# A hybrid decoder trunk: SBUF buffers shared out anew, S5 products on another engine, one weight sum formed later

## The chip, the core and the metric

The kernel runs on one core of a Trainium2 chip. The metric is the device time of one execution in microseconds; three runs were taken. TensorE (PE) does the matmuls, VectorE (DVE) and ScalarE (ACT) the element-wise work, GpSimd (POOL) some more of it, and SyncE (SP) issues most of the DMAs, in one queue and in program order.

## The reference, cut to what matters

One layer: one projection of x, (1024, 2048), to all branches, three mixers, and one projection back, with a residual and LayerNorm.

```python
h = jnp.einsum('bld,dn->bln', x, w_in[l])
(s5_u, s5_z, ml_qk, ml_v, ml_i, ml_f, ml_o, ml_z, ssd_xbc, ssd_dt, ssd_z) = split_in(h)
y_s5 = s5_mixer(s5_u, ...) * jax.nn.silu(s5_z.astype(f32))
qk = jax.nn.silu(causal_dwconv(ml_qk, ml_conv_w[l], ml_conv_b[l]))
y_ml = mlstm_mixer(q, k, ml_v, ...) * jax.nn.silu(ml_z.astype(f32))
xbc = jax.nn.silu(causal_dwconv(ssd_xbc, ssd_conv_w[l], ssd_conv_b[l]))
y_ssd = rms_norm(ssd_mixer(xs, bs, cs, ...) * jax.nn.silu(ssd_z.astype(f32)), ssd_norm_g[l])
mixed = jnp.concatenate([y_s5, y_ml, y_ssd], axis=-1)
x = layer_norm(DEEPNORM_ALPHA * x + jnp.einsum('bln,nd->bld', mixed, w_out[l]), ln_g[l], ln_b[l])
```

The S5 mixer is a complex diagonal recurrence over time, s(t) = lam_bar * s(t-1) + B u(t), computed here in batches of states with complex numbers as pairs of real rows.

## The kernel before, in words

**Products.** Every fp32 operand of a projection is split in two fp32r parts: `split` (L178 to L180) casts it on ScalarE (names ending in h) and subtracts on VectorE (names ending in l). A product takes three matmuls: h by h, h by l, l by h. A weight tile is `w<n>`, numbered in the order of use: raw `w<n>r`, parts `w<n>h` and `w<n>l`.

**The block** (`block`, about 0 to 720 us) does a part of the input projection by a scheme of block products over the two halves of rows and of contraction, of Strassen's kind: seven products instead of eight, on sums of blocks. First come the token-major weights, in five stages, (1), (2), (5, 6), (3, 7) and (4), for three groups of columns of which the first and third are `w_gt`. A stage's piece is `unit` (L1371): one weight tile of 256 rows, two steps k of 128 rows, four tiles of tokens, 24 matmuls of 128x512. After it come the channel-major weights `w_c` (the columns, about 480 to 720 us), in the order `CSEQ`. Weights w24 to w31 are the first group's of stage (5, 6), w72 to w75 the same group's in stage (4). Operand sums of x (`xc`, `xd`, `xe`, parts `p..`) are formed beside them, and `tick` puts other work between units: the S5 mixer's constants and then its eight batches `s5m0` to `s5m7` (`s5_batch`, L1040), one step of a generator at a time.

**Weight sums.** A sum is a `Chain`: `raw` loads the first block (`w24r`), `mix` (L231) loads another (`w24q`) and adds or subtracts it on VectorE in place. `right` (L1169) says which blocks each product needs. With `early` true, product 6's chain subtracts a further block after its split and stores the result in DRAM (`tg`), from where product 4 takes it ready; with `early` false the store comes before, and product 4 loads tg and the further block and subtracts there. Before, `early` is true for the first of the three groups (`g == 0`).

**Buffers.** All raw loads, weights, sums and operands alike, take turns in `NR` = 5 buffers ("wr", 4 KB per partition), which a load may enter once the buffer's last reader is done. Tiles made by `gt` take turns in `NG` = 24 buffers of 2 KB ("g"). Both pools last for the whole kernel. The block's accumulators lie in `zp`, 23 buffers of 2 KB, and the 24th takes one of "g" (L1294).

**Order.** Each engine takes its instructions in the order in which the program's builder put them, and the builder places them by when it thinks buffers and data come free: the counts of buffers shift the order on every queue, SP's above all.

**After the block** come two halves of the tokens (`half`: conv, mLSTM, SSD), and an output projection after each, whose second operand is loaded as `y0r` and `y1r` through the same raw buffers, one per weight tile at first. x's second half is loaded as `x1r`.

Of the kernel before, what the change touches and what calls it, by code (L numbers as in the profile page):

```python
# [17 lines left out]
P = 128  # L18
# [6 lines left out]
QSC = 96.0 ** -0.5  # L25
NEG = -1.0e30
NWARM = 8
NG = 24
NR = 5


_W = dict(ssd_conv_w=56, ssd_conv_b=14, ml_conv_w=24, ml_conv_b=6, ssd_d=6, ssd_norm_g=6, ml_norm_g=6, s5_b_glu=4, s5_lre=32, s5_lim=32, s5_lst=32)
# [7 lines left out]
def hybrid_trunk(ctx: ExitStack, tc: tile.TileContext, a: dict, out: bass.AP, dbg=None):  # L40
# [3 lines left out]
    cp = ctx.enter_context(tc.tile_pool(name="cp", bufs=1))  # L44
    xp = ctx.enter_context(tc.tile_pool(name="xp", bufs=8))
    wp = ctx.enter_context(tc.tile_pool(name="wp", bufs=3))
    gp = ctx.enter_context(tc.tile_pool(name="gp", bufs=NG))
    pj = ctx.enter_context(tc.tile_pool(name="pj", bufs=4, space=PSUM))
    mx = ctx.enter_context(tc.tile_pool(name="mx", bufs=4, space=PSUM))
    dr = ctx.enter_context(tc.tile_pool(name="dr", bufs=1, space=DRAM))  # L50
# [6 lines left out]
    def gt(name, shape=(P, HT), dtype=F32):  # L57
        return gp.tile(list(shape), dtype, name=name, tag="g")
# [109 lines left out]
    bg = Background()  # L168


    warm = gt("warm", dtype=BF16)
    dve.memset(warm, 0.0)
    wps = mx.tile([P, HT], F32, name="warmp", tag="mx")
    for _ in range(NWARM):
        pe.matmul(wps, lhsT=warm[:, 0:P], rhs=warm, start=True, stop=True)
# [6 lines left out]
    class Tokens:  # L182
# [5 lines left out]
        def load(self, kk):  # L188
            assert kk == len(self.h)
            if self.early:  # L190
                self.load_early(kk)
                return
            r = wp.tile([P, 2, HT], F32, name=f"{self.nm}r{kk}", tag="wr", bufs=NR)
            sync.dma_start(out=r, in_=self.src(kk))
            th = xp.tile([P, 2, HT], F32R, name=f"{self.nm}h{kk}", tag="xh")
            tl = xp.tile([P, 2, HT], F32R, name=f"{self.nm}l{kk}", tag="xl")
            split(r, th, tl)
            self.h.append(th)
            self.l.append(tl)
# [13 lines left out]
            self.l.append(tl)  # L213

    def raw(src, shape, n):
        r = wp.tile(list(shape), F32, name=n, tag="wr", bufs=NR)
        sync.dma_start(out=r, in_=src)
        return r

# [15 lines left out]
    class Weights:  # L235
# [34 lines left out]

        def begin(self):
            src, shape = self.plan[self.at]
            r = wp.tile(list(shape), F32, name=f"w{self.at}r", tag="wr", bufs=NR)
            self.first = src, (r, *self.parts())
            self.ready.append(self.first[1][1:])

# [762 lines left out]
    def s5_batch(sb, gT, ctx_):  # L1039
        n = f"s5m{sb}"  # L1040
        bt, hf = sb // 2, sb % 2

        def ld(nm):
            t_ = gt(n + nm)
            sync.dma_start(out=t_, in_=s5d[nm][sb])
            return t_

        def ld_half(nm, r0):

            t_ = gt(n + nm)  # L1050
# [24 lines left out]
        for g in range(4):
            pe.matmul(A[:, g * P:(g + 1) * P], lhsT=R[:, g * P:(g + 1) * P], rhs=U[:, g * P:(g + 1) * P], start=True, stop=True)
        As = gt(n + "As")
        act.mul(As[0:64], A[64:128], -1.0)
        act.copy(out=As[64:128], in_=A[0:64])
        v, v2 = gt(n + "v"), gt(n + "v2")  # L1080
        dve.tensor_mul(out=v, in0=A, in1=T0)
        pool.tensor_mul(out=v2, in0=As, in1=T1)
        dve.tensor_add(out=v, in0=v, in1=v2)
        w = gt(n + "w")
        dve.tensor_tensor_scan(out=w, data0=rt.rearrange("p q j -> p (q j)"), data1=v, initial=0.0, op0=ALU.mult, op1=ALU.add)
        yield
        ws = gt(n + "ws")
        act.mul(ws[0:64], w[64:128], -1.0)
        act.copy(out=ws[64:128], in_=w[0:64])
        x1, x2, X = gt(n + "x1"), gt(n + "x2"), gt(n + "X", (P, 4, P))  # L1090
        v3 = lambda t_: t_.rearrange("p (q j) -> p q j", q=4)[:, :, 0:P - 1]
        dve.tensor_mul(out=x1, in0=w, in1=T0)
        pool.tensor_mul(out=x2, in0=ws, in1=T1)
        pool.memset(X[:, :, 0:1], 0.0)
        dve.tensor_sub(out=X[:, :, 1:P], in0=v3(x1), in1=v3(x2))
        O = ld("O")
        M = gt(n + "M", (P, 8, 64))
        K = s5d["K"]
        for t in range(8):
            sync.dma_start(out=M[:, t, :], in_=K[16 * t:16 * t + P, 64 * sb:64 * sb + 64])  # L1100
        yield
        yield
        ps = pm(n + "y")
        for g in range(4):
            sl = slice(g * P, (g + 1) * P)
            pe.matmul(ps[:, sl], lhsT=X[:, g, :], rhs=O[:, sl], start=True, stop=False, skip_group_check=True)
            pe.matmul(ps[:, sl], lhsT=U[:, sl], rhs=M[:, :, 16 * g:16 * g + 16], start=False, stop=True, skip_group_check=True)
        if hf == 0:
            ctx_["Y"] = [gt(n + f"Y{i}", (P, 4, P)) for i in range(2)]
        Y = ctx_["Y"]  # L1110
        for i in range(2):
            act.copy(out=Y[i][:, :, 64 * hf:64 * hf + 64].rearrange("p t (g c) -> p g t c", g=4),
                     in_=ps.rearrange("p (g t c) -> p g t c", g=4, t=8)[:, :, 4 * i:4 * i + 4, :])
        yield
        if hf == 1:

            for i in range(2):
                ps = pm(n + f"g{i}")
                for x in range(4):
                    pe.transpose(ps[:, (3 - x) * P:(4 - x) * P], Y[i][:, x, :], ident)  # L1120
                lo = 4 - 4 * i
                for h in range(2):
                    act.activation(out=gT[bt][h].rearrange("p (j t) -> p t j", t=8)[:, lo:lo + 4, :],
                                   in_=ps.rearrange("p (t j) -> p t j", t=4)[:, :, 64 * h:64 * h + 64], func=AF.Gelu_apprx_tanh)
            yield
# [65 lines left out]

    w_t = [lambda c, u, g=g: a["w_gt"][g, c, u] for g in range(2)]
    w_t.insert(1, lambda c, u: a["w_gv"][c, u])
    wt = [[right(lambda k, c, g=g, u=u: w_t[g](c, 4 * k + u), (P, 2, GN[g]), f"tg{g}{u}", g == 0) for u in range(4)] for g in range(3)]
    wc = [right(lambda k, c, p=p: a["w_c"][p[c], k], (P, 8, P), f"cg{p[0]}", j > 2) for j, p in enumerate(GC)]
    STAGES = ((1,), (2,), (5, 6), (3, 7), (4,))

# [94 lines left out]
    def block():  # L1292
# [6 lines left out]

        def new(n):  # L1300
            count.append(n)
            return gt(n) if len(count) == 24 else zp.tile([P, HT], F32, name=n, tag="state")

        def plus(o, x, y, op=add):
            dve.tensor_tensor(out=o, in0=x, in1=y, op=op)  # L1305
# [65 lines left out]
        def unit(i, X, g, u, ps, w):  # L1371
            wh, wl = w
            N = GN[g]
            order = [(t, k) for t in range(4) for k in range(2)] if u in (0, 3) else [(t, k) for k in range(2) for t in range(4)]
            for t, k in order:
                K = 2 * u + k
                s_h, s_l = X.h[u][:, k, t * P:(t + 1) * P], X.l[u][:, k, t * P:(t + 1) * P]
                pe.matmul(ps[t][:, 0:N], lhsT=s_h, rhs=wh[:, k, :], start=(K == 0), stop=False)
                pe.matmul(ps[t][:, 0:N], lhsT=s_h, rhs=wl[:, k, :], start=False, stop=False)
                pe.matmul(ps[t][:, 0:N], lhsT=s_l, rhs=wh[:, k, :], start=False, stop=(K == 7))  # L1380
                if K == 7:
                    evac_t(i, g, t, ps[t])
            tick()
# [231 lines left out]

    mixsrc = lambda h: lambda kk: mixT[kk * 256:(kk + 1) * 256, h * HT:(h + 1) * HT].rearrange("(two p) n -> p two n", p=P)
    X = [Tokens(lambda kk, h=h: a["xT"][h, kk], f"x{h}") for h in range(2)] + [Tokens(mixsrc(h), f"y{h}") for h in range(2)]
    with tc.tile_pool(name="zp", bufs=23) as zp:
        X[0] = block()
    sp = ctx.enter_context(tc.tile_pool(name="sp", bufs=2))  # L1620
    hp = ctx.enter_context(tc.tile_pool(name="hp", bufs=1))
    st_s = hp.tile([P, 768], F32, name="st_s")
# [96 lines left out]
```

## Time and profile before

| | |
|---|---|
| median of three runs | 1634.3 us (1633.9 to 1637.83) |
| the profiled execution | 1636.77 us, span 1634.8 us |
| mean granted clock of TensorE | 0.988 |
| busy: PE, DVE, ACT, POOL | 97%, 68%, 40%, 6% of the span |
| DMA | 333.56 MB, mean 204 GB/s |

The page's busy shares say which engine fills the span. The windows say, by stretch, how long each engine was busy and which clock TensorE was granted. The list of waits names the instruction for which an engine stood, and what it stood for. The timeline gives single instructions in order, with the idle time before each in brackets.

### The profile page before, as it was taken

Reading aid. Unit: us, or ns where it says so; the run is one execution under the profiler, and the core shown is the slowest. Engines: PE = TensorE matmul, PEld = TensorE weight load, DVE = VectorE, ACT = ScalarE, POOL = GpSimd, SP = SyncE. Lnnn points to the kernel's source line nnn. Section 1 sums busy time; section 2 is a strip of 40 time slices with the busy share of each in tenths; the row PEclk is TensorE's granted clock in tenths of the full one; section 3 lists DMA queues with packets and bytes.
Section 4 is the critical chain, followed back from the end, with each engine's and each line's share of the span. In section 5 each row is a group of like instructions: output and inputs, shape, how many; then the busy total and the mean of one; then the engine's idle time right before and its main releaser. Section 6 shows DMA issues by size and latency. Waiting matters only on the chain. (4 is left out here: it accounts for less than half of the span.)

```text
span 1634.8 us, 21170 instructions
## 1 busy us (share of the span) xinstructions
PE 1589.8 (97%) x7688; PEld 1334.9 (82%) x7688; DVE 1116.1 (68%) x1828; ACT 658.1 (40%) x927; POOL 97.0 (6%) x199
## 2 busy tenths in 40 slices
PE   9998999999999899999999999999999999999996
PEld 7886898897888778887888888878888888888885
DVE  4668977878867766656655888776588763484348
ACT  4432233127444554644443356455444431322122
POOL 0000000000003230001110001010000000000000
PEclk9999999999999999999999999999999999999998
DMA  8887886986897767664523663443565454575444
GB/s 298 309 280 245 285 289 237 321 285 211 290 310 246 255 196 247 218 225 144 155 94 113 195 194 120 143 161 97 180 200 161 135 185 128 183 235 166 121 140 164
DMA packets 139303, 333.56 MB, mean 204 GB/s; under 512 B 24488, under 2 KB 41000, under 8 KB 139200
## 3 DMA queue, kind: packets, MB, share of 16 engines
q1 hardware_dynamic: 129792, 317.54, 59.1%
q10 hardware_dynamic: 9408, 14.68, 2.6%
q8 instruction: 60, 0.98, 0.2%
q14 instruction: 43, 0.35, 0.1%
HBM read 271.74 MB, written 57.28 MB: 201 GB/s over the span
## 5 line engine op out<-in xcount | busy, mean ns | idle before, releaser
L1305 DVE TENSOR_TENSOR e<-e,b 128x512 f32<-128x512 f32 (+1 forms) x72 | 43.6, 643 | 6.0 <-PE b L1380 5.9
L180 DVE TENSOR_TENSOR y1l<-y1r,y1h 128x1024 fp32r<-128x1024 f32 x8 | 9.8, 1224 | 21.8 <-ACT y1h L179 21.8
L1565 DVE SCALAR_TENSOR_TENSOR r<-r,lrs,ln_b 128x512 f32<-128x512 f32 x32 | 23.0, 740 | 0.0
L1564 DVE SCALAR_TENSOR_TENSOR r<-r,mv,ln_g 128x512 f32<-128x512 f32 x32 | 22.9, 736 | 0.0
L370 ACT ACT_TABLE_LOAD x15 | 19.2, 1283 | 5.5 <-DVE xb16cv L369 3.8
L1584 DVE BATCH_NORM_STATS2 bst<-r 128x6 f32<-128x512 f32 x32 | 20.7, 681 | 0.0
L1060 POOL COPY s5m0up<-s5m0u 128x256 f32<-128x256 f32 x2 | 1.1, 532 | 329.7 <-DMA s5m0u<-s5u 329.7
L179 ACT CAST y1h<-y1r 128x1024 fp32r<-128x1024 f32 x8 | 8.4, 1054 | 28.2 <-PE op03p L352 28.2
L1305 DVE TENSOR_TENSOR f<-f,b1c 128x512 f32<-128x512 f32 x15 | 9.4, 682 | 8.7 <-ACT f L1358 8.7
L1285 ACT ACTIVATE f<-f 128x512 f32<-128x512 f32 x20 | 12.1, 628 | 6.6 <-DVE f L1305 3.2
L1305 DVE TENSOR_TENSOR f<-f,b37c 128x512 f32<-128x512 f32 x10 | 6.4, 683 | 10.2 <-PE b37c L1452 10.2
L1305 DVE TENSOR_TENSOR f<-f,b2c 128x512 f32<-128x512 f32 x5 | 3.4, 687 | 11.6 <-PE b2c L1452 11.6
L787 DVE TENSOR_TENSOR s5small<-s5small 128x32 f32<-128x32 f32 (+2 forms) x66 | 10.9, 193 | 0.5
L1556 ACT ACTIVATE lrs<-lrs 128x1 f32<-128x1 f32 x8 | 1.6, 203 | 23.7 <-DVE lrs L1555 23.7
L1168 DVE TENSOR_TENSOR gsg<-gsg,gsz 128x512 f32<-128x512 f32 x8 | 5.4, 691 | 8.0 <-DMA gsz<-s5z 7.9
L749 PEld LDWEIGHTS mf<-ident,sgo 128*128 128x128 f32 x48 | 5.7, 140 | 5.8 <-DVE sgo L739 5.0
L739 DVE TENSOR_TENSOR sgo<-sgo,mzs 128x384 f32<-128x384 f32 x16 | 8.9, 554 | 2.3 <-DMA mzs<-zg 2.0
L1279 ACT ACT_TABLE_LOAD x8 | 10.3, 1283 | 0.1
L749 PE MATMUL mf<-ident,sgo 128*128 128x128 f32 x48 | 8.9, 281 | 1.4 <-DVE sgo L739 1.3
L180 DVE TENSOR_TENSOR y0l<-y0r,y0h 128x1024 fp32r<-128x1024 f32 x8 | 9.7, 1218 | 0.3 <-ACT y0h L179 0.3
L1278 ACT ACT_TABLE_LOAD x7 | 9.0, 1283 | 2.4 <-ACT e L1279 2.4
L1322 ACT COPY e<-b 128x512 f32<-128x512 f32 (+1 forms) x12 | 6.6, 556 | 8.1 <-PE b L1380 8.1
(4692 smaller groups left out, 5765.5 us busy)
## 6 DMA issues: line engine op xcount, KB each, us to landing
xn<-in_x_dram SPq DMA_DIRECT2D x32, 256.0 KB, 5.7
out_dram<-r SPq DMA_DIRECT2D x32, 256.0 KB, 2.7
x1r<-in_xT_dram SPq DMA_DIRECT2D x8, 512.0 KB, 3.5
y0r<-mixT SPq DMA_DIRECT2D x8, 512.0 KB, 3.5
y1r<-mixT SPq DMA_DIRECT2D x8, 512.0 KB, 3.3
vd<-e SPq DMA_DIRECT2D x16, 192.0 KB, 4.2
szd<-f ACTq DMA_DIRECT2D x12, 256.0 KB, 2.7
vx<-vd SPq DMA_DIRECT2D x8, 384.0 KB, 4.0
```

The costliest lines, as they stand in the source:

```text
L180: dve.tensor_sub(out=tl, in0=raw, in1=th.bitcast(F32))
L370: act.activation(out=dest, in_=c, func=AF.Silu)
L739: dve.tensor_mul(out=sg, in0=sg, in1=sz)
L749: pe.transpose(pt[:, c * P:(c + 1) * P], hg[c][t // 3][:, (t % 3) * P:(t % 3 + 1) * P], ident)
L787: eng.tensor_tensor(out=o, in0=i, in1=j, op=op)
L1278: act.activation(out=c[:, 0:256], in_=c[:, 0:256], func=AF.Silu)
L1279: act.activation(out=c[:, 256:512], in_=c[:, 256:512], func=AF.Sigmoid)
L1285: act.activation(out=c, in_=c, func=AF.Silu)
L1305: dve.tensor_tensor(out=o, in0=x, in1=y, op=op)
L1564: dve.scalar_tensor_tensor(out=o, in0=o, scalar=mv[:, 0:1], in1=lng[nb], op0=ALU.subtract, op1=ALU.mult)
L1565: dve.scalar_tensor_tensor(out=o, in0=o, scalar=rs, in1=lnb[nb], op0=ALU.mult, op1=ALU.add)
L1584: dve.bn_stats(out=st[t][:, nb, :], in_=r[t][nb])
```

## The change

- The pools "g" and "wr" are made anew for the block and for what follows. Per partition the block has 22 g buffers (44 KB), 7 raw ones (28 KB) and 21 accumulators (42 KB), before 24, 5 and 23 (48, 20 and 46 KB): 114 KB in both. What follows has 27 g buffers and 3 raw ones (54 and 12 KB), before 24 and 5 (48 and 20 KB).
- Three accumulators instead of one lie in "g".
- The two products of `s5_batch` that GpSimd formed, `v2` and `x2`, 128x512 each, go to VectorE: 16 instructions in eight batches.
- `right` gets `early` false for all token-major weights: the fourth block is not subtracted in stage (5, 6) but in stage (4), four loads of 512 KB and four subtractions.
- In the very first unit the four token tiles take turns at the first k, then at the second; before, each token tile did both k before the next.
- The warm-up matmuls move into the block's `with`.

The core of the diff:

```diff
-NG = 24
-NR = 5
+NGB, NRB, NZ = 22, 7, 21
+NGH, NRH = 27, 3
...
-    gp = ctx.enter_context(tc.tile_pool(name="gp", bufs=NG))
...
-            r = wp.tile([P, 2, HT], F32, name=f"{self.nm}r{kk}", tag="wr", bufs=NR)
+            r = rw.tile([P, 2, HT], F32, name=f"{self.nm}r{kk}", tag="wr")
...
-        pool.tensor_mul(out=v2, in0=As, in1=T1)
+        dve.tensor_mul(out=v2, in0=As, in1=T1)
...
-        pool.tensor_mul(out=x2, in0=ws, in1=T1)
+        dve.tensor_mul(out=x2, in0=ws, in1=T1)
...
-    wt = [[right(lambda k, c, g=g, u=u: w_t[g](c, 4 * k + u), (P, 2, GN[g]), f"tg{g}{u}", g == 0) for u in range(4)] for g in range(3)]
+    wt = [[right(lambda k, c, g=g, u=u: w_t[g](c, 4 * k + u), (P, 2, GN[g]), f"tg{g}{u}", False) for u in range(4)] for g in range(3)]
...
-            return gt(n) if len(count) == 24 else zp.tile([P, HT], F32, name=n, tag="state")
+            return gt(n) if NZ < len(count) <= 24 else zp.tile([P, HT], F32, name=n, tag="state")
...
-            order = [(t, k) for t in range(4) for k in range(2)] if u in (0, 3) else [(t, k) for k in range(2) for t in range(4)]
+            order = [(t, k) for t in range(4) for k in range(2)] if u == 3 or u == 0 and (i, g) != (1, 0) else [(t, k) for k in range(2) for t in range(4)]
...
-    with tc.tile_pool(name="zp", bufs=23) as zp:
+    with tc.tile_pool(name="gb", bufs=NGB) as gp, tc.tile_pool(name="rb", bufs=NRB) as rw, tc.tile_pool(name="zp", bufs=NZ) as zp:
...
         X[0] = block()
+    gp = ctx.enter_context(tc.tile_pool(name="gh", bufs=NGH))
+    rw = ctx.enter_context(tc.tile_pool(name="rh", bufs=NRH))
```

**TensorE's first unit.** The piece begins with the second matmul; `b_<n>` are the four token tiles' accumulators, and a tile's three matmuls of one k are h by h, l and then l by h. Before:

```order
L1378 MATMUL b100_164<-w0h_171,p1h0_168 128x512
L1379 MATMUL b100_164<-w0l_172,p1h0_168 128x512
L1378 MATMUL b101_165<-w0h_171,p1h0_168 128x512
L1379 MATMUL b101_165<-w0l_172,p1h0_168 128x512
L1380 MATMUL b100_164<-w0h_171,p1l0_169 128x512
L1378 MATMUL b100_164<-w0h_171,p1h0_168 128x512
L1380 MATMUL b101_165<-w0h_171,p1l0_169 128x512
L1378 MATMUL b101_165<-w0h_171,p1h0_168 128x512
L1378 MATMUL b102_166<-w0h_171,p1h0_168 128x512
L1379 MATMUL b100_164<-w0l_172,p1h0_168 128x512
L1380 MATMUL b100_164<-w0h_171,p1l0_169 128x512
L1379 MATMUL b101_165<-w0l_172,p1h0_168 128x512
```

Now:

```order
L1370 MATMUL b100_167<-w0h_174,p1h0_171 128x512
L1371 MATMUL b100_167<-w0l_175,p1h0_171 128x512
L1370 MATMUL b101_168<-w0h_174,p1h0_171 128x512
L1371 MATMUL b101_168<-w0l_175,p1h0_171 128x512
L1372 MATMUL b100_167<-w0h_174,p1l0_172 128x512
L1372 MATMUL b101_168<-w0h_174,p1l0_172 128x512
L1370 MATMUL b102_169<-w0h_174,p1h0_171 128x512
L1371 MATMUL b102_169<-w0l_175,p1h0_171 128x512
L1372 MATMUL b102_169<-w0h_174,p1l0_172 128x512
L1370 MATMUL b103_170<-w0h_174,p1h0_171 128x512
L1371 MATMUL b103_170<-w0l_175,p1h0_171 128x512
L1372 MATMUL b103_170<-w0h_174,p1l0_172 128x512
```

Before, the first tile's second k stood as its sixth matmul; now all four tiles' first k comes first, twelve matmuls.

**SP in stage (5, 6).** `w24r`, `w26r` are first blocks, `w24q..`, `w26q..` the further ones, `xe..` operand sums, `tg..` the stores of weight sums, `vd` stores of results. Before:

```order
L217 DMA p62r_1198<-xs62_154 128x1024
L217 DMA w24r_1204<-in_w_gt_dram 128x1024
L217 DMA w24q0_1206<-in_w_gt_dram 128x1024
L217 DMA p63r_1253<-xs63_158 128x1024
L217 DMA w24q1_1267<-in_w_gt_dram 128x1024
L217 DMA w24q2_1274<-in_w_gt_dram 128x1024
L217 DMA w26r_1278<-in_w_gt_dram 128x1024
L217 DMA w26q0_1280<-in_w_gt_dram 128x1024
L217 DMA xe0r_1359<-xs60_146 128x1024
L217 DMA xe0q0_1361<-in_xT_dram 128x1024
L233 DMA tg00_128<-w24r_1204 128x1024
```

Now:

```order
L1263 DMA vd_111<-e211_1048 128x384
L1263 DMA vd_111<-e212_1058 128x384
L209 DMA w24r_1207<-in_w_gt_dram 128x1024
L1263 DMA vd_111<-e213_1068 128x384
L209 DMA w24q0_1209<-in_w_gt_dram 128x1024
L209 DMA p63r_1256<-xs63_144 128x1024
L209 DMA w24q1_1270<-in_w_gt_dram 128x1024
L209 DMA w26r_1278<-in_w_gt_dram 128x1024
L209 DMA w26q0_1280<-in_w_gt_dram 128x1024
L209 DMA xe0r_1359<-xs60_132 128x1024
L209 DMA xe0q0_1361<-in_xT_dram 128x1024
```

The load `w24q2` is gone, `w26r` follows `w24q1`, `tg00` is stored earlier, and the stores `vd` have come to stand around `w24r`.

**SP in the columns, at the third and fourth S5 batch.** `p7..` are operand parts, `s5m..` the batches' constants and data (`M` is eight transfers). Before:

```order
L217 DMA w94r_4615<-in_w_c_dram 128x1024
L1045 DMA s5m3R_4612<-s5R_107 128x512
L217 DMA p70r_4648<-xs70_148 128x1024
L217 DMA p71r_4654<-xs71_152 128x1024
L217 DMA p72r_4660<-xs72_156 128x1024
L217 DMA p73r_4666<-xs73_160 128x1024
L1045 DMA s5m2O_4693<-s5O_108 128x512
L1100 DMA s5m2M_4695<-s5K_110 128x64 x8
L1052 DMA s5m3T0_4711<-s5T_109 64x512 x2
L1052 DMA s5m3T1_4714<-s5T_109 64x512 x2
L217 DMA w95r_4721<-in_w_c_dram 128x1024
L217 DMA w94q0_4792<-in_w_c_dram 128x1024
```

Now:

```order
L225 DMA cg24_130<-w91r_4411 128x1024
L209 DMA p71r_4657<-xs71_138 128x1024
L209 DMA p72r_4663<-xs72_142 128x1024
L1037 DMA s5m3R_4615<-s5R_104 128x512
L209 DMA p73r_4669<-xs73_146 128x1024
L209 DMA w95r_4724<-in_w_c_dram 128x1024
L209 DMA w94q0_4795<-in_w_c_dram 128x1024
L1037 DMA s5m2O_4696<-s5O_105 128x512
L1092 DMA s5m2M_4698<-s5K_107 128x64 x8
L1044 DMA s5m3T0_4714<-s5T_106 64x512 x2
L1044 DMA s5m3T1_4717<-s5T_106 64x512 x2
L209 DMA w95q0_4879<-in_w_c_dram 128x1024
```

`w95r` and `w94q0` now stand ahead of `s5m2O`, `s5m2M` and `s5m3T`, before behind them; `w94r` and `p70r` have gone further ahead, before `s5m1O`, `s5m1M` and `s5m2T`, and so are not in the second piece.

## Rows read from the trace of the kernel before

**Rows 1.** The page, part 1: busy us, share of the span, instructions
```profile
PE 1589.8 (97%) x7688; PEld 1334.9 (82%) x7688; DVE 1116.1 (68%) x1828; ACT 658.1 (40%) x927; POOL 97.0 (6%) x199
```

**Rows 2.** Windows of 40 us: engines' busy us (x instructions), granted clock, DMA share, GB/s
```profile
0.00:40.00 40.00, 36.62 (x155) 29.50 (x156) 19.12 (x23) 17.88 (x25) 2.46 (x17) 0.96 0.85 296
40.00:80.00 40.00, 40.00 (x187) 34.55 (x186) 23.94 (x43) 16.51 (x20) 0.96 (x3) 1.00 0.88 314
...
120.00:160.00 40.00, 33.89 (x135) 25.99 (x134) 31.17 (x72) 11.84 (x13) 0.25 (x2) 0.91 0.72 247
160.00:200.00 40.00, 37.73 (x166) 31.57 (x166) 38.55 (x128) 11.44 (x15) 0.00 (x0) 0.96 0.85 290
...
360.00:400.00 40.00, 37.17 (x168) 30.55 (x168) 28.22 (x36) 24.30 (x29) 0.00 (x0) 0.96 0.71 238
400.00:440.00 40.00, 40.00 (x204) 35.78 (x203) 34.24 (x44) 25.25 (x31) 0.00 (x0) 1.00 0.79 256
...
520.00:560.00 40.00, 34.76 (x175) 28.64 (x174) 31.19 (x32) 22.16 (x33) 9.65 (x14) 0.96 0.81 264
...
600.00:640.00 40.00, 36.42 (x177) 30.52 (x176) 30.62 (x32) 19.85 (x28) 9.39 (x10) 0.91 0.65 209
1440.00:1480.00 40.00, 40.00 (x178) 33.14 (x177) 38.03 (x62) 10.94 (x14) 0.00 (x0) 1.00 0.78 257
```

**Rows 3.** A window of 4 us, same columns
```profile
144.00:148.00 4.00, 3.05 (x8) 2.35 (x8) 3.98 (x5) 0.00 (x0) 0.00 (x0) 0.50 0.41 135
```

**Rows 4.** TensorE's waits, four of the largest: us in total, times, longest
```profile
PE b L1378 <- ACT w26h L179: 4.2, 1, 4.2
PE b37c L1450 <- ACT w103h L179: 3.1, 1, 3.1
PE b L1378 <- ACT w70h L179: 2.6, 1, 2.6
...
PE cu0cs L405 <- DVE gt1f L386: 1.5, 1, 1.5
```

**Rows 5.** Timeline of TensorE, 6 to 9 us: start, us, line, output<-inputs, idle before
```profile
8.40 0.80 PE L1378 MATMUL b<-w0h,p1h 128*128 128x512 f32 x1 [1.56 <-ACT w0h L179]
```

**Rows 6.** Timeline of SP from 130 us, then of VectorE at 140 us
```profile
130.53 0.33 SPq L217 DMA_DIRECT2D w26r<-in_w_gt_dram  x1
132.86 0.33 SPq L217 DMA_DIRECT2D w26q<-in_w_gt_dram  x1
...
140.08 1.23 DVE L231 TENSOR_TENSOR w26r<-w26r,w26q 128x1024 f32<-128x1024 f32 x1 [3.74 <-DMA w26q<-in_w_gt_dram]
```

**Rows 7.** Timeline of SP, 530 to 542 us
```profile
530.82 7.62 SPq L1100 DMA_DIRECT2D s5m2M<-s5K  x8
...
541.02 0.53 SPq L217 DMA_DIRECT2D w95r<-in_w_c_dram  x1
```

**Rows 8.** Timeline of VectorE at 603 us
```profile
603.34 1.79 DVE L231 TENSOR_TENSOR w101r<-w101r,w101q 128x1024 f32<-128x1024 f32 x1
```

**Rows 9.** Lines 1082 and 1081: durations in ns, least, median, most
```profile
L1082 POOL TENSOR_TENSOR s5m2v<-s5m2As,s5m2T x1: 1291/1291/1291, 527.7 to 527.7; 128x512 f32<-128x512 f32 x1
...
L1081 DVE TENSOR_TENSOR s5m2v<-s5m2b,s5m2T x1: 684/684/684, 526.4 to 526.4; 128x512 f32<-128x512 f32 x1
```

**Rows 10.** Timeline of SP at 1427 us, then the tile w233r
```profile
1427.05 0.33 SPq L217 DMA_DIRECT2D w235r<-in_w_out_dram  x1
...
L179 ACT CAST w233h<-w233r x1: 1052/1052/1052, 1424.5 to 1424.5; 128x1024 fp32r<-128x1024 f32 x1
L180 DVE TENSOR_TENSOR w233l<-w233r,w233h x1: 1216/1216/1216, 1425.8 to 1425.8; 128x1024 fp32r<-128x1024 f32 x1
...
DMA to landing us min/median/max: 5.2/5.2/5.2
```

**Rows 11.** Timeline of TensorE at 1445 us
```profile
1445.14 0.39 PE L353 MATMUL op03p<-w234h,y0l 128*128 128x512 f32 x1
1445.37 0.39 PE L351 MATMUL op10p<-w235h,y1h 128*128 128x512 f32 x1
```

More of the change, by code (lines that the diff above doesn't have):

```diff
@@ L168, in hybrid_trunk @@
     bg = Background()
[L171 to L175, printed above, removed]
     def split(raw, th, tl):
@@ L215, in raw @@
     def raw(src, shape, n):
-        r = wp.tile(list(shape), F32, name=n, tag="wr", bufs=NR)
+        r = rw.tile(list(shape), F32, name=n, tag="wr")
         sync.dma_start(out=r, in_=src)
@@ L272, in begin @@
             src, shape = self.plan[self.at]
-            r = wp.tile(list(shape), F32, name=f"w{self.at}r", tag="wr", bufs=NR)
+            r = rw.tile(list(shape), F32, name=f"w{self.at}r", tag="wr")
             self.first = src, (r, *self.parts())
@@ L1617, in hybrid_trunk @@
     X = [Tokens(lambda kk, h=h: a["xT"][h, kk], f"x{h}") for h in range(2)] + [Tokens(mixsrc(h), f"y{h}") for h in range(2)]
-    with tc.tile_pool(name="zp", bufs=23) as zp:
+    with tc.tile_pool(name="gb", bufs=NGB) as gp, tc.tile_pool(name="rb", bufs=NRB) as rw, tc.tile_pool(name="zp", bufs=NZ) as zp:
+        warm = gt("warm", dtype=BF16)
+        dve.memset(warm, 0.0)
+        wps = mx.tile([P, HT], F32, name="warmp", tag="mx")
+        for _ in range(NWARM):
+            pe.matmul(wps, lhsT=warm[:, 0:P], rhs=warm, start=True, stop=True)
         X[0] = block()
+    gp = ctx.enter_context(tc.tile_pool(name="gh", bufs=NGH))
+    rw = ctx.enter_context(tc.tile_pool(name="rh", bufs=NRH))
     sp = ctx.enter_context(tc.tile_pool(name="sp", bufs=2))
```

## The prediction

> **What bounds the kernel now.** I read the page's shares first: TensorE works 97% of the span, the next engine 68% [rows 1]. So only two things can give time back without taking matmuls away, and none is taken away here: TensorE's idle stretches, and stretches in which it works at half its clock. The windows of 40 us show both at once [rows 2]. A window's loss is 40 less its PE time, plus 40 times what its granted clock lacks of 1.00. That gives 120 to 160: 6.1 + 3.6 = 9.7 us; 160 to 200: 2.3 + 1.6 = 3.9; 360 to 400: 2.8 + 1.6 = 4.4; 520 to 560: 5.2 + 1.6 = 6.8; 600 to 640: 3.6 + 3.6 = 7.2. The first window holds warm-up and first loads; its avoidable part is one wait of 1.56 us [rows 5] and 1.6 of clock, 3.2 together. The level behind the 0.9s is half: 0.50, 1.2 GHz, right after the wait at 138 [rows 3]. A window under 1.00 is seen only where TensorE had stood for over 1.5 us, so such a wait costs nearly double. All of this lies in the block and its columns; the list of waits names the instructions TensorE stood for [rows 4]: splits of weights (w26h, w70h, w103h) that came late, and one wait at the start of the halves (cu0cs).
>
> **The sum, part by part.** It is made against the profiled execution, 1636.8 us, which is 2.5 above the median of the three runs (1634.3).
>
> *First unit in k order.* TensorE did 5 matmuls, then stood 1.56 us for the second half of w0 until 8.40 [rows 5]. Now 7 more of the first half come before it. Two neighbouring matmuls start 0.23 us apart [rows 11], so 7 x 0.23 = 1.6 fill that wait. **Gain 1.5**; ends 0 (the next split late instead) and 3.2 (the half clock goes too).
>
> *Stage (5,6): seven raw buffers, and no early sum.* w26r was issued at 130.53 and w26q at 132.86, and the mix of w26 stood 3.74 us for w26q [rows 6]; TensorE then waited 4.2 for w26h [rows 4]. A unit is 24 matmuls, 24 x 0.23 = 5.5 us, and a pair of units 10.9. Before, a pair took 6 raw buffers (r, three q, and two of an operand sum), one per 1.8 us. Two buffers more let a load start 3.6 us earlier, and the one load fewer per pair (w24q2, w26q2 and so on) another 1.8: 5.4 together, over the 4.2 waited for. On SP, w26r now follows w24q1 directly, without w24q2 between. So I take the idle time of 120 to 160 down by 5.4 of 6.1, and with it the clock's 3.6: **gain 9.0**; ends 0 and 9.7. In 160 to 200 VectorE works 38.6 of 40 us [rows 2]; four subtractions of 1.23 us [rows 6] leave this stage, 4.9 us, but it stays nearly full. I take half of the 3.9: **gain 2.0**; ends 0 and 3.9.
>
> *Stage 4 takes that work over:* 4 loads of 512 KB and 4 x 1.23 = 4.9 us of VectorE. It works 34.2 of 40 us in 400 to 440 [rows 2], which makes 39; in 360 to 400 it has 11.8 us free, and three of the four subtractions now stand ahead of w70l, where these are. w70h itself stays late, since ScalarE's chain ahead of it is unchanged: 4.4 us stay. **Loss 1.5**, about one subtraction too late; ends 0 and 4.9.
>
> *Columns, 480 to 640.* SP stood on the eight s5m2M transfers and two s5m3T from 530.82 until it issued w95r at 541.02 [rows 7]; TensorE's 5.2 us of idle time in 520 to 560 follow from w94 and w95. Now w95r and w94q stand ahead of s5m2O and s5m2M on SP, and w94l ahead of the s5m2 chain on VectorE. But that chain now has an instruction on VectorE that waits for ScalarE (s5m2As, s5m2ws), with p71l to p73l and w95l queued behind it. I take two thirds of 6.8: **gain 4.5**; ends 0 and 6.8.
>
> *At 603* the mix of w101 came behind s5m6v and took 1.79 us beside GpSimd's work [rows 8], where 1.23 is usual [rows 6]; TensorE stood 3.1 for w103h behind it [rows 4]. In the new order w101q is issued ahead of w104r and the mix stands before p42l. **Gain 5.0** of 7.2, since the S5 chain there changes places too; ends 0 and 7.2.
>
> *The 16 products.* On GpSimd 1.29 us each, on VectorE 0.68 for the twin product [rows 9]: 16 x 0.68 = 10.9 us more on VectorE, spread over 160 us of which 30.6 to 31.2 of each 40 are taken [rows 2]. The cover is some 9 us per window against 2.7 added; without it, 10.9 would show. **0.**
>
> *Into the halves.* cu0cs stood 1.5 us for gt1f [rows 4]. Now the halves' first tiles come from new pools that lie where the block's did, so the copy that fills gt0LC also waits for the last stores from old g tiles. **Loss 1.5**, the same wait twice; ends -1.5 and 3.
>
> *Three raw buffers in the halves:* **0**, costed in the third rival.
>
> Sum: -1.5 - 9.0 - 2.0 + 1.5 - 4.5 - 5.0 + 1.5 = -19.0. That is 1617.8 against the profiled execution, 1615.3 against the median.
>
> **The rivals.**
>
> *1. The columns only trade waits.* SP is one queue: what moves ahead pushes s5m2O, s5m2M and s5m3T back, and TensorE takes the S5 matmuls in program order. Then the 9.5 us of columns and 603 come back under other names. For: SP has no slack there [rows 7]. Against: each S5 batch has two units between its loads and its matmuls. 1615.3 + 9.5 = **1624.8**.
>
> *2. Stage (5,6) does not start its loads earlier.* Either SP stands elsewhere (four vd stores, which wait for evacuations, now stand directly around w24r), or the transfers are limited by rate. The four pairs of units moved 4 x (4 loads + 2 operand loads + 1 store) = 28 x 512 KB = 14.7 MB in 43.6 us, 337 GB/s; now 24, 289 GB/s. The highest 40 us of the rows is 314 [rows 2], so by the rows the old stage asked for more than was ever held and the new one for a little less: rate may still bind at its densest pair. Both windows concerned moved only 247 and 290, though. Without these 11.0: **1626.3**. The Trainium skill (DMA: Bandwidth & Descriptors, Specifications) puts the HBM limit of a core at about 358 GB/s; no row of 40 us here reaches it. By that the old demand would fit too, rate would be no cause, and the rival would rest on SP's order alone, with 0.06 in place of 0.10; the sum would be the same.
>
> *3. Three raw buffers starve the second output projection: slower.* There w and y1 loads alternate, two per unit. w235r was issued at 1427.05 and needed at 1445.37 [rows 10, 11], 18.3 us. Two buffers fewer take one unit, 5.5, so 12.9 are left; landing (5.2), cast (1.05) and subtraction (1.22) take 7.5 [rows 10]: 5.4 of slack. Three buffers serve two loads per 5.5 us as long as a buffer's turn is under 8.2 us. If splits wait behind the LayerNorm work on VectorE (38.0 of 40 us in 1440 to 1480 [rows 2]), and a turn takes 12 us, a unit lasts 8.0, and 8 units lose 8 x 2.5 - 5.4 = 15 us. The loads of x1 and y0 alternate with weights in the same way; at the same price the three stretches cost 45, so 1615.3 + 45 = **1660**. It decides from a turn of 9.2 us on (8 x 0.67 = 5.4), and the whole is slower than before from about 10.7. Against: 7.5 us is what the rows show of a turn, and among the largest waits cu0cs is the only one in the halves [rows 4].
>
> *4. Every wait named goes, and no new one comes:* 3.2 + 9.7 + 3.9 + 6.8 + 7.2 = 30.8, **1603.5**.
>
> **How the numbers follow.** 0.3% (4.9 us) is about what a measurement can tell from no change, so "same" is 1629.4 to 1639.2. Forecast 0.44; rival 4, 0.10; rival 1 alone, 0.16; rival 2 alone, 0.10: all faster, 0.80. Rivals 1 and 2 together leave -19 + 20.5 = +1.5, 1635.8: same, 0.11. Rival 3 and the like: slower, 0.09. Range 1602 to 1634: rival 4 and the ends of its terms below, rivals 1 and 2 above, and the lower part of "same".
>
> **What would show it.** Right: no wait for w26h or w33h over 1 us and a clock of 1.00 in 120 to 200; w70h still 2 to 3 us; columns with under 3 us of idle time in 520 to 560 and in 600 to 640; GpSimd without the products and VectorE 16 instructions of 0.68 us richer; halves without a wait for weights. Wrong: waits of PE for s5m tiles, or w72 to w75, over 2 us; a wait for y1 or w2xx in the output projections; or the clock still at half between 140 and 150.

## The result, and the profile after

The changed kernel takes 1613.1 us (median of four runs, 1610.0 to 1615.2) where the kernel before, in its four runs, takes 1636.1 (1633.9 to 1641.1). The ratio is 0.9854, with a 95% interval of 0.9824 to 0.9884: 23 us faster, 19 to 29. The forecast was 1615.3. The profiled execution took 1610.04 us, span 1608.3; that is 3 us below its median, so the two profiled executions stand 26.7 us apart, a little more than the medians do.

The page, part 1:

```profile
PE 1579.1 (98%) x7688; PEld 1329.4 (83%) x7688; DVE 1120.7 (70%) x1844; ACT 658.2 (41%) x927; POOL 80.3 (5%) x183
```

TensorE is busy for 98% of a shorter span, where [rows 1] has 97%. The windows of 40 us that answer to [rows 2], in the same columns; since the program has become shorter, what stood in 600 to 640 stands in 560 to 600 now:

```profile
0.00:40.00 40.00, 38.41 (x170) 31.55 (x171) 21.07 (x25) 19.51 (x27) 2.46 (x17) 1.00 0.88 319
...
120.00:160.00 40.00, 40.00 (x178) 32.92 (x177) 34.76 (x70) 13.08 (x14) 0.25 (x2) 1.00 0.88 313
160.00:200.00 40.00, 40.00 (x207) 37.89 (x206) 39.00 (x145) 11.46 (x16) 0.00 (x0) 1.00 0.73 256
...
360.00:400.00 40.00, 36.50 (x169) 29.91 (x168) 32.38 (x43) 29.32 (x36) 0.00 (x0) 0.91 0.74 234
...
520.00:560.00 40.00, 39.52 (x213) 33.47 (x212) 32.14 (x37) 21.47 (x34) 7.32 (x10) 1.00 0.70 232
560.00:600.00 40.00, 38.96 (x209) 32.91 (x208) 32.31 (x37) 19.80 (x29) 6.63 (x10) 1.00 0.71 232
600.00:640.00 40.00, 40.00 (x194) 33.57 (x193) 28.51 (x33) 26.44 (x37) 0.10 (x1) 1.00 0.81 275
```

The 9.7 and 3.9 us lost in 120 to 200 are gone, and in 120 to 160 DMA moves 313 GB/s instead of 247. Of the columns' losses 0.5 and 1.0 us are left. 360 to 400 has become worse: PE 36.5 of 40 us at a clock of 0.91, before 37.2 at 0.96. TensorE's waits, answering to [rows 4]:

```profile
PE cu0cs L397 <- DVE gt1f L378: 1.9, 1, 1.9
PE b L1370 <- ACT w70h L171: 1.8, 1, 1.8
PE b L1371 <- DVE w70l L172: 1.7, 1, 1.7
...
PE op00p L343 <- ACT xb113st L355: 1.1, 1, 1.1
PE s5m7b L1068 <- ACT s5m7U L1060: 1.0, 1, 1.0
```

w26h and w103h are gone from the list, cu0cs has grown from 1.5 to 1.9, and at w70 TensorE now stands twice, 1.8 us for ScalarE's part and then 1.7 for VectorE's (before 2.6 and 0.3).

For the comparisons below the span is cut at the first matmul that reads a given weight: w0 begins the first column, w24 stage (5, 6), w48 (3, 7), w84 the columns, w124 the first half, w203 the first output projection. These lengths are worked out from the starts of those matmuls in each trace; half clock and waits are both in them. There is one trace per kernel, and kernels that do the same in a stretch can still differ there: by 2 us to w24 (122.7 to 124.7 in those with the new first unit) and by 5 from w124 to w203 (523.5 to 528.8 in those with 3 raw buffers after the block). In us:

| kernel | to w24 | w24 to w48 | w48 to w84 | w84 to w119 | w124 to w203 | w203 to PE's end |
|---|---|---|---|---|---|---|
| before | 125.8 | 137.0 | 200.1 | 237.0 | 524.7 | 362.7 |
| after | 123.3 | 122.4 | 201.2 | 223.4 | 525.7 | 365.1 |
| pools alone | 124.3 | 122.2 | 198.4 | 227.2 | 523.5 | 365.6 |
| block's pools undone | 124.5 | 124.8 | 208.1 | 232.6 | 524.5 | 365.2 |
| late sum alone | 128.0 | 125.0 | 206.1 | 235.6 | 524.4 | 362.7 |
| early sum again | 123.2 | 122.2 | 200.7 | 223.5 | 528.8 | 364.6 |
| products on GpSimd | 122.8 | 122.9 | 203.4 | 225.9 | 524.8 | 363.8 |
| the same, M later | 124.6 | 123.8 | 201.9 | 224.7 | 523.5 | 364.8 |
| first unit as before | 125.5 | 122.3 | 203.0 | 223.5 | 524.0 | 364.5 |
| 5 raw after the block | 123.0 | 122.2 | 202.7 | 224.2 | 524.7 | 362.8 |
| 2 raw after the block | 124.4 | 122.6 | 202.0 | 223.5 | 529.4 | 370.9 |
| early sum, tables | 122.7 | 122.2 | 196.4 | 223.5 | 524.5 | 365.6 |
| early sum, 5 raw | 123.5 | 122.2 | 199.5 | 223.5 | 522.1 | 363.1 |
| early sum, tables, 5 raw | 124.7 | 122.2 | 196.5 | 223.5 | 522.8 | 362.7 |

w119 to w124 takes 27.2 us in all of them. The change's 26.6 us to TensorE's end are -2.5, -14.6, +1.1, -13.6, +1.0 and +2.4, and 0.4 ahead of w0's first matmul and by rounding. The +1.0 lies within the scatter of its stretch. The tail behind TensorE, 14.8 us before, is 14.9.

### The profile page after: what moved, and what is told of

Its sections match the earlier page's. It is cut to its first block, busy times and chain, and to the rows that moved or that the text cites. A ratio compares the mean times of both kernels' runs of the same rounds, so it can differ in the third digit from the quotient of the medians.

```text
span 1608.3 us, 21146 instructions
## 1 busy us (share of the span) xinstructions
PE 1579.1 (98%) x7688; PEld 1329.4 (83%) x7688; DVE 1120.7 (70%) x1844; ACT 658.2 (41%) x927; POOL 80.3 (5%) x183
## 5 line engine op out<-in xcount | busy, mean ns | idle before, releaser
L172 DVE TENSOR_TENSOR x1l<-x1r,x1h 128x1024 fp32r<-128x1024 f32 x8 | 9.8, 1219 | 2.3 <-ACT x1h L171 2.3
L171 ACT CAST y0h<-y0r 128x1024 fp32r<-128x1024 f32 x8 | 8.4, 1046 | 4.9 <-PE xbc_13p L1531 4.8
```

## The experiments

Each edit is to the changed kernel unless it says otherwise, and each ratio is to the kernel before, run beside it.

**The pools alone.** The kernel before with the new pools and nothing else; as an edit of the changed kernel:

```diff
-f"tg{g}{u}", False)
+f"tg{g}{u}", g == 0)
-dve.tensor_mul(out=v2, in0=As, in1=T1)
+pool.tensor_mul(out=v2, in0=As, in1=T1)
-dve.tensor_mul(out=x2, in0=ws, in1=T1)
+pool.tensor_mul(out=x2, in0=ws, in1=T1)
-if u == 3 or u == 0 and (i, g) != (1, 0) else
+if u in (0, 3) else
```

> The kernel before with the new pools alone: early sum, products on GpSimd and first unit as before. Theory A: the start loses 3.3 us again, 120 to 200 some 1 to 4 (the fourth load a pair is back), columns 0 to 4, w70 gains 1 to 3: 1615 to 1621. Theory B: columns lose 8 to 13 more: 1624 to 1632.

Measured: 1613.5 us, ratio 0.9866 (0.9843 to 0.9890). That is a little under theory A's range. The pools alone do what the whole change does, as far as times can tell. In 120 to 200 nothing is lost again, although the fourth load a pair is back. The other parts don't do nothing, though: by medians the products and the first unit give 6 us and the late sum takes 5.6 back, as the run with the sum formed early again shows below. And the pools are three counts changed together (raw, g and accumulators); that it is the two raw buffers which help is argued from the loads, not shown by a run of its own.

**The block's pools undone.**

```diff
-NGB, NRB, NZ = 22, 7, 21
+NGB, NRB, NZ = 24, 5, 23
```

> The changed kernel with the block's pools as before (24 g, 5 raw, 23 accumulators); the three other parts of the change stay. Theory A (the raw buffers bring the loads forward, and with them SP's order in the columns): the waits in 120 to 200 and in 520 to 640 come back, less the one load a pair that is gone: 138 stands 2 to 4 us, columns and 603 lose 8 to 13 us in all; 1628 to 1636 us. Theory B (the products' move to VectorE clears the columns): only 120 to 200 loses again, 6 to 13 us, the columns stay free; 1619 to 1626.

Measured: 1626.9 us, ratio 0.9950 (0.9933 to 0.9968); 14 us of the 23 go, and the time lies between the ranges of the two theories. Theory A holds for the columns, 9.2 us longer than in the changed kernel, and falls for stage (5, 6), which stays good with five buffers: 124.8 us. Neither theory had the 6.9 us that w48 to w84 loses, where TensorE stands at w70, w74 and w80. The list of TensorE's waits of this run:

```profile
PE b3c L1442 <- ACT w95h L171: 4.1, 1, 4.1
PE b L1370 <- ACT w70h L171: 3.3, 1, 3.3
...
PE b L1371 <- DVE w25l L172: 1.7, 1, 1.7
PE b L1371 <- DVE w74l L172: 1.6, 1, 1.6
...
PE b37c L1442 <- ACT w103h L171: 1.4, 1, 1.4
```

w95h and w103h are back, w25l's 1.7 us is all that stage (5, 6) has, and w70 and w74 are worse than in either kernel.

**The late sum alone.** An edit of the kernel before:

```diff
-f"tg{g}{u}", g == 0)
+f"tg{g}{u}", False)
```

> The kernel before with the fourth weight sum not formed early, and nothing else. If the one load fewer a pair relieves stage (5, 6) by itself, as the run with five raw buffers suggests: the waits in 120 to 200 fall from 8 us to under 2.5 and the clock stays at 1.00 there, w70 grows by 1 to 2, columns and 603 as before; 1621 to 1628. Rival (there the relief came from another part of the change): waits of 4 us and more at 138, 1632 to 1636.

Measured: 1630.3 us, ratio 0.9967 (0.9955 to 0.9979), a little over the range; the theory's place was right and the total too hopeful. Stage (5, 6) goes from 137.0 to 125.0, and w48 to w84 from 200.1 to 206.1: half of what one stage gains the other pays. The first unit's wait for w0h, 2.4 us here, takes another 2.2. So in stage (5, 6) either part of the change is enough: 137.0 with neither, 125.0 with the late sum, 122.2 with the pools, 122.4 with both. The line of the tile w26r that forms its sum (duration in ns, then the start in us) shows how far each brings that sum forward; before, it began at 140.08 [rows 6]. With the late sum alone, then the pools alone (the first of two starts), then both:

```profile
L231 DVE TENSOR_TENSOR w26r<-w26r,w26q x1: 1227/1227/1227, 135.2 to 135.2; 128x1024 f32<-128x1024 f32 x1
```

```profile
L223 DVE TENSOR_TENSOR w26r<-w26r,w26q x2: 1219/1222/1225, 124.6 to 144.0; 128x1024 f32<-128x1024 f32 x2
```

```profile
L223 DVE TENSOR_TENSOR w26r<-w26r,w26q x1: 1224/1224/1224, 121.6 to 121.6; 128x1024 f32<-128x1024 f32 x1
```

5 us by the load that is gone, 15 by the pools. The loads themselves move less. SP's timeline has w26r and w26q, before at 130.53 and 132.86 [rows 6], with the late sum alone at

```profile
128.05 0.33 SPq L217 DMA_DIRECT2D w26r<-in_w_gt_dram  x1
131.60 0.33 SPq L217 DMA_DIRECT2D w26q<-in_w_gt_dram  x1
```

and with the pools alone at

```profile
117.73 0.33 SPq L209 DMA_DIRECT2D w26r<-in_w_gt_dram  x1
120.97 0.33 SPq L209 DMA_DIRECT2D w26q<-in_w_gt_dram  x1
```

So the missing load brings them forward by 2.5 and 1.3 us; the rest of its 5 us is that w26q lands after 3.5 us, where it took 7.1 before. The pools bring them forward by 12.8 and 11.9.

**The sum formed early again.**

```diff
-f"tg{g}{u}", False)
+f"tg{g}{u}", g == 0)
```

> The changed kernel with the fourth weight sum formed early again in stage (5, 6). If the load a pair that was taken out mattered (my step: 1.8 of the 5.4 us), 120 to 200 shows waits of 0.5 to 3 us for w26 to w33; if seven buffers alone suffice, none. In stage (4) the wait for w70l (1.7 us, behind the mix of w74 on VectorE) goes and w70h's stays at 1.8 to 2.8. Sum -4 to +4: 1609 to 1617.

Measured: 1607.5 us, ratio 0.9833 (0.9806 to 0.9860). The median is 5.6 us below the changed kernel's, the intervals overlap. That is below the expected range. No wait for w26 to w33: seven buffers suffice. And w70l's wait is gone, as expected. The first two lines of this run's list of TensorE's waits, among which w70l has only 0.2 us:

```profile
PE mf L741 <- DVE sgo L731: 2.8, 4, 1.0
PE b L1370 <- ACT w70h L171: 2.7, 1, 2.7
```

What it comes from stands in VectorE's timeline of the changed kernel:

```profile
368.77 1.23 DVE L223 TENSOR_TENSOR w74r<-w74r,w74q 128x1024 f32<-128x1024 f32 x1 [5.02 <-DMA w74q<-in_w_gt_dram]
...
372.99 1.22 DVE L172 TENSOR_TENSOR w70l<-w70r,w70h 128x1024 fp32r<-128x1024 f32 x1
```

The subtraction for w74, one of the four that were moved, stood 5.02 us at the head of VectorE's queue for its load, with five other instructions and then w70l in the queue behind it; w70l's input w70h had been ready since 371.03. In all six runs with seven buffers and the late sum w70l's wait is 1.3 to 2.8 us, in the three with the early sum and the tables untouched 0.2 or 0.3. With 5 raw buffers after the block (below) the same comparison is clearer: 1603.3 us with the early sum, 1608.8 with the late one, and no run of the one reaches the other. So by times the late sum costs some 5.5 us with seven buffers. The wait at w70l is a part of that only: w48 to w84 is longer by 0.5 us in the one pair of traces and by 3.2 in the other, and where the rest lies is not shown.

**The products back on GpSimd, and then M's loads later.**

```diff
-dve.tensor_mul(out=v2, in0=As, in1=T1)
+pool.tensor_mul(out=v2, in0=As, in1=T1)
-dve.tensor_mul(out=x2, in0=ws, in1=T1)
+pool.tensor_mul(out=x2, in0=ws, in1=T1)
```

> The changed kernel with the 16 S5 products back on GpSimd. Theory A: the columns keep their loads ahead of S5's, so at most the mix at w101 is slow again beside GpSimd; 0 to 4 us lost, 1613 to 1617. Theory B: the waits for w94, w95 and w103 are back, 8 to 13 us; 1621 to 1626.

Measured: 1615.9 us, ratio 0.9885 (0.9859 to 0.9911): theory A by time, but one wait of theory B is there.

```profile
PE b3c L1442 <- ACT w95h L171: 3.3, 1, 3.3
```

The timeline of SP in this run, and then in the changed kernel, shows why:

```profile
514.63 7.42 SPq L1092 DMA_DIRECT2D s5m2M<-s5K  x8
522.16 2.54 SPq L1044 DMA_DIRECT2D s5m3T<-s5T  x4
524.75 0.58 SPq L209 DMA_DIRECT2D w95r<-in_w_c_dram  x1
```

```profile
510.57 0.87 SPq L209 DMA_DIRECT2D w95r<-in_w_c_dram  x1
511.53 0.69 SPq L209 DMA_DIRECT2D w94q<-in_w_c_dram  x1
...
513.18 7.02 SPq L1092 DMA_DIRECT2D s5m2M<-s5K  x8
```

With the products on VectorE the builder puts w95r ahead of s5m2O and s5m2M; with them on GpSimd it stands behind, and comes 14 us later, though M's loads stand only 1.5 us apart in the two runs. To tell SP's order from GpSimd's own delay, the next run keeps the products on GpSimd and lets each batch's loads of O and M follow one step later:

```diff
+        yield
         O = ld("O")
         M = gt(n + "M", (P, 8, 64))
...
         yield
-        yield
```

> The changed kernel with the products back on GpSimd, as in the run that lost 3.3 + 0.8 us at w95, but each S5 batch's loads of O and M issued one step later, so that w95r stands ahead of s5m2O and s5m2M on SP. Theory C (w95 waits because SP stands on the eight M transfers ahead of its load): w95r is issued some 7 us earlier, the waits for w95h and w95l fall under 1.5 us, and with the clock 3 to 6 us come back: 1610 to 1613. Rival (the product on GpSimd itself makes VectorE and ScalarE late): the wait stays at 3 us or more, 1616.

Measured: 1613.1 us, ratio 0.9869 (0.9852 to 0.9886). Its runs overlap those of the run before, so the times don't decide; by the waits both are at work. Now SP issues w95r 6 us earlier, ahead of M:

```profile
518.64 0.34 SPq L209 DMA_DIRECT2D w95r<-in_w_c_dram  x1
...
523.95 4.99 SPq L1093 DMA_DIRECT2D s5m2M<-s5K  x8
```

That is still 8 us behind the changed kernel. The wait for w95h halves, from 3.3 to 1.6 us. But 1.7 us for w94l are new, and VectorE's timeline names GpSimd:

```profile
518.73 1.10 DVE L1087 TENSOR_TENSOR s5m2X<-s5m2x,s5m2x 128x508 f32<-128x508 f32 x1 [2.01 <-POOL s5m2X L1086]
519.75 1.21 DVE L172 TENSOR_TENSOR w94l<-w94r,w94h 128x1024 fp32r<-128x1024 f32 x1
```

s5m2X stood 2.01 us for GpSimd's product and its memset, with w94l behind it. The stage takes 224.7 us, against 225.9 and, with the products on VectorE, 223.4.

**The first unit as before.**

```diff
-if u == 3 or u == 0 and (i, g) != (1, 0) else
+if u in (0, 3) else
```

> The changed kernel with the first unit's order as before. Theory: TensorE stands 1.0 to 1.6 us for the second half of w0 at 7 us again, and the clock's 1.7 may come back with it; nothing else changes, so 1614 to 1617 us. Rival (the start is hidden, since the next splits come no earlier): the wait moves behind the first unit and the time stays at 1613.

Measured: 1613.7 us, ratio 0.9866 (0.9837 to 0.9895). The times can't tell it from the changed kernel; the trace can. The wait is back, and the stretch to w24 takes 2.2 us more:

```profile
9.18 0.51 PE L1370 MATMUL b<-w0h,p1h 128*128 128x512 f32 x1 [2.88 <-ACT w0h L171]
```

The 2.2 us are no clean price, because the start varies from trace to trace, also where no edit touches it. In the changed kernel three of w0's first matmuls stand 0.4 to 0.6 us apart before the pace of 0.23 is reached, in "early sum, tables, 5 raw" eleven, in this run none.

**Five and two raw buffers after the block.**

```diff
-NGH, NRH = 27, 3
+NGH, NRH = 23, 5
```

> The changed kernel with 23 g and 5 raw buffers after the block in place of 27 and 3. If three raw buffers cost nothing, as I forecast: the same within 2 us, and the 0.4 us wait for w274h at the end goes. If they starve the output projections: over 3 us faster. If the 27 g buffers are what counts in the halves: slower, with new waits there.

Measured: 1608.8 us, ratio 0.9839 (0.9806 to 0.9872), by medians 4 us below the changed kernel, the intervals overlapping. The traces agree with each other: from w203 to TensorE's end all five kernels with 5 raw buffers there take 362.7 to 363.1 us, all eight with 3 take 363.8 to 365.6. In this run the waits for w274h and xb113st are gone. The g buffers change with the raw ones, from 27 to 23, and no run separates the two.

```diff
-NGH, NRH = 27, 3
+NGH, NRH = 29, 2
```

> The changed kernel with 29 g and 2 raw buffers after the block. My working: three serve two loads a unit up to a buffer's turn of 8.2 us, two up to 5.5, while the rows show 7.5. So two must starve the stretches in which weights and operand loads alternate: 8 units of 7.5 in place of 5.5, 16 us less some 5 of lead in each of three, 20 to 40 us slower, with waits of TensorE for w and y splits around them; 1633 to 1653. Rival (the turn is shorter than I think, or the lead longer): under 10 us slower.

Measured: 1621.1 us, ratio 0.9912 (0.9885 to 0.9939): 8 us over the changed kernel, so the rival, not my working. The starvation is there, but small. TensorE's timeline at the first matmul that needs each unit's subtracted part:

```profile
1407.82 0.50 PE L344 MATMUL op03p<-w232l,y0h 128*128 128x512 f32 x1 [0.76 <-DVE w232l L172]
...
1413.87 0.50 PE L344 MATMUL op03p<-w233l,y0h 128*128 128x512 f32 x1 [0.28 <-DVE w233l L172]
...
1419.78 0.50 PE L344 MATMUL op03p<-w234l,y0h 128*128 128x512 f32 x1 [0.18 <-DVE w234l L172]
...
1426.19 0.50 PE L344 MATMUL op10p<-w235l,y1h 128*128 128x512 f32 x1 [0.63 <-DVE w235l L172]
```

The units take 6.1, 5.9 and 6.4 us in place of 5.5. One buffer's turn can be followed in the timelines of SP, ScalarE and VectorE:

```profile
1407.79 0.33 SPq L209 DMA_DIRECT2D w233r<-in_w_out_dram  x1
...
1413.85 0.33 SPq L209 DMA_DIRECT2D w234r<-in_w_out_dram  x1
...
1411.51 1.05 ACT L171 CAST w233h<-w233r 128x1024 fp32r<-128x1024 f32 x1 [1.97 <-DMA w233r<-in_w_out_dram]
...
1412.59 1.23 DVE L172 TENSOR_TENSOR w233l<-w233r,w233h 128x1024 fp32r<-128x1024 f32 x1 [1.80 <-ACT w233h L171]
```

From w233r's issue to its cast 3.7 us, then the cast and the subtraction, and the next load is issued at 1413.85: a turn of 6.1 us, not 7.5. The steps do follow one another; it is the landing that was too long. I had taken the 5.2 us of one load [rows 10], w233r before, which was a slow one: the y1r loads beside it have a median of 3.3.

**The table loads grouped, and the best version.** What is left at w70h is ScalarE's chain in the changed kernel: Silu and Sigmoid of one tile after another, each with its own table load, up to w70h's cast:

```profile
364.71 1.28 ACT L1270 ACT_TABLE_LOAD   x1 [0.39 <-ACT e L1271]
...
366.44 1.28 ACT L1271 ACT_TABLE_LOAD   x1
...
369.98 1.05 ACT L171 CAST w70h<-w70r 128x1024 fp32r<-128x1024 f32 x1
```

The edit does the four tiles' Silu as they come and their Sigmoid together at the end:

```diff
             act.activation(out=c[:, 0:256], in_=c[:, 0:256], func=AF.Silu)
-            act.activation(out=c[:, 256:512], in_=c[:, 256:512], func=AF.Sigmoid)
             act.dma_start(out=zg[rows, HT:768], in_=c[:, 0:256])
-            act.dma_start(out=og[rows, HT:768], in_=c[:, 256:512])
+            late.append((c, rows))
+            if t == 3:
+                for c_, rows_ in late:
+                    act.activation(out=c_[:, 256:512], in_=c_[:, 256:512], func=AF.Sigmoid)
+                    act.dma_start(out=og[rows_, HT:768], in_=c_[:, 256:512])
+                late.clear()
```

With the early sum:

> The sum formed early again, and ScalarE's Silu and Sigmoid of the last group of stage (3, 7) and its kin grouped by function over the four token tiles (two table loads in place of eight). Theory: w70h waits for ScalarE's chain of eight table loads of 1.28 us, so six fewer bring it 7.7 us forward; the wait of 2.7 us at w70h and the clock's 1.7 go, against the run with the early sum alone 3 to 5 us faster: 1602 to 1605. Rival (the wait only passes to w70l, behind other work on VectorE): 0 to 2 us.

Measured: 1607.8 us, ratio 0.9826 (0.9798 to 0.9855), level with the early sum alone, so the rival, although the wait for w70h is gone and w48 to w84 takes 196.4 us instead of 200.7: w70l keeps a wait of 1.7, and the scatter of these four runs (1604.2 to 1609.5) is as large as the expected gain. With 5 raw buffers after the block the runs lie closer. First without the grouping:

> The changed kernel with the sum formed early again and 23 g and 5 raw buffers after the block. If the two runs' gains add: 2 to 5 us for each, 1602 to 1607. If the second was noise: 1607.

Measured: 1603.3 us (1602.4 to 1604.7), ratio 0.9802 (0.9788 to 0.9817). The two gains add. Then with it (the three edits together):

> As the run before, with ScalarE's table loads grouped as well. The wait for w70h (2.7 us and 1.7 of clock) goes: 2 to 5 us below the run before, 1599 to 1605, if the trace's own account holds; level with it if w70l takes the wait over.

Measured: 1600.9 us (1600.0 to 1601.5), ratio 0.9786 (0.9772 to 0.9801). No run of the one reaches the other. This version beats both kernels: 35 us under the one before, 12 under the changed one. Its largest wait but the warm-up's, and w70l's, in the list of TensorE's waits:

```profile
PE ms L571 <- DVE sm L566: 1.2, 1, 1.2
...
PE b L1377 <- DVE w70l L172: 0.6, 1, 0.6
```

The window of 360 to 400, where the changed kernel has 36.50 us of PE at 0.91:

```profile
360.00:400.00 40.00, 39.36 (x181) 32.34 (x180) 33.69 (x44) 23.25 (x32) 0.00 (x0) 1.00 0.78 242
```

## Why the prediction was right, point by point

The forecast of the likeliest case was 2.2 us over the result; its sum, -19.0, compares with -26.7 between the profiled executions and -23 between medians. Most gains were taken too small, and one loss was left out.

- **The first unit**, gain 1.5: the wait went, and the clock of 0.96 in 0 to 40 with it; 2.5 us to w24, between the value taken and the upper end. How much of that is the new order is open, since the slow pace at the start varies from trace to trace. And "such a wait costs nearly double" does not hold for every wait: in the run with the first unit as before TensorE stood 2.88 us and the granted clock of 0 to 40 is 1.00, and in the changed kernel cu0cs's 1.9 us leave it at 1.00 in 680 to 720.
- **Stage (5, 6)**, gain 9.0 + 2.0: 14.6. The mechanism, loads that come earlier by two buffers and by one load fewer, is shown by the runs. The step that failed is its size: "Two buffers more let a load start 3.6 us earlier, and the one load fewer per pair another 1.8". The second was about right, 1.3 to 2.5 us; the pools brought w26's loads forward by 12 to 13. Most of that lead had been gathered in the stages before: w24r, the stage's first load, was issued at 107.9 us with the pools alone, at 118.7 before and at 120.1 with the late sum alone. My rate of one buffer per 1.8 us held for a pair of units of this stage and was applied to loads that start ahead of it. I added the two where either one was enough. The half I withheld in 160 to 200, since VectorE is full there, was not needed: it works 39.0 of 40 us, and TensorE doesn't wait.
- **Stage 4**, loss 1.5: w48 to w84 lost 1.1. I had the place, subtractions ahead of w70l, but not the reason. "In 360 to 400 it has 11.8 us free" counted free time, and missed that VectorE stands in order: the subtraction for w74 waited 5.02 us of that time for its load, and w70l came behind it. With five raw buffers the loss is 6 to 8 us (the late sum alone, the block's pools undone), so that here it is small is also the pools' doing.
- **Columns and 603**, gain 4.5 + 5.0: 13.6, close to the full 14.0. The pools alone give 9.8 of it and clear 603; the products' move gives the rest, by SP's order and by GpSimd's delay. The queue that I feared behind s5m2As cost 0.5 us at most, the wait for w95l that is left.
- **The 16 products**, 0: their cover held, and beyond that they earned 2.5 us (225.9 against 223.4).
- **Into the halves**, loss 1.5: cu0cs grew by 0.4 only. In the other kernels with the new pools it is 1.8 us or less, in some nothing, so that the pools' place is its cause is not shown.
- **Three raw buffers**, 0: here the term was mis-sized. They cost 2.4 us from w203 on, which the run with five (and 23 g) gives back.

Rival 2 is out: with pools and early sum the same 28 transfers a stage cause no wait, and the changed kernel moves 313 GB/s in 120 to 160. Rate was not the bound. The highest 40 us of the after trace have 326, but a window of 16 us shows what the core can move:

```profile
8.00:24.00 16.00, 16.00 (x71) 12.92 (x70) 10.60 (x14) 8.59 (x13) 0.00 (x0) 1.00 1.01 392
```

The Trainium skill gives about 358 GB/s as the HBM limit of a core (DMA: Bandwidth & Descriptors, Specifications). The trace's 392 over 16 us lie above it, and the measurement decides: in this program 358 was no limit. Rival 1 happened at one wait only (s5m7b, 1.0 us). Rival 3's mechanism is real and shows from two buffers on, but at 8 us, where I expected 20 to 40 of two buffers and 45 of three. Rival 4 was nearest of the four, since most waits went and the clock went with them.

What stays open: why the runs of one kernel scatter by 5 us where the halves have three raw buffers and by 2 where they have five and the sum is early (1610.0 to 1615.2 against 1602.4 to 1604.7).

## What to carry to other kernels

Where loads take turns in a pool, don't size the gain of more buffers by the rate at which one stage asks for them: the larger pool brought w26's loads forward by more than three times what that rate said (12 to 13 us against 3.6), because the lead gathers over the stages before. Parts of a change that remove the same wait don't add; undo each alone, and drop the one that only moves work, as the late sum does here. Free time of an in-order engine is no cover for an instruction that has to wait for a load: whatever stands behind it waits too.

## What the runs showed of the hardware that was not expected

VectorE's 16 products take 11.4 us by their durations in the trace of the changed kernel, but it is busy for only 5.9 us more than in the run with the products on GpSimd (1120.7 against 1114.8 us):

```profile
PE 1579.6 (98%) x7688; PEld 1330.7 (83%) x7688; DVE 1114.8 (69%) x1828; ACT 659.0 (41%) x927; POOL 96.4 (6%) x199
```

Of the 5.5 us between, 2.9 are the overlap of neighbouring instructions in the profile's times, and 2.5 net are other instructions of VectorE that had been longer. Most of that is the subtraction that forms s5m0X to s5m7X. With the products on GpSimd six of the eight took 1.10 us:

```profile
L1087 DVE TENSOR_TENSOR s5m2X<-s5m2x,s5m2x x1: 1101/1101/1101, 517.4 to 517.4; 128x508 f32<-128x508 f32 x1
```

With them on VectorE six took 0.67 to 0.69 and two 0.87 and 0.88. What GpSimd did beside the six long ones was no product but a copy of 0.61 us (`s5m3rho` here), so the order of the queues put the two together. Beside the products a few instructions were long too, like the 1.79 us of [rows 8], while others took their usual 0.68. The Trainium skill (GPSIMD Engine Reference, Key points) says that GpSimd shares its SBUF interfaces with VectorE and contends with VectorE instructions that have two SBUF inputs. The trace agrees: the subtraction has two, and each of the six lost 0.4 us.
